# The MLP of a hybrid decoder block: token sums formed from PSUM while the tokens are transposed, three early column pairs, and the down accumulators in the memory of two token sums

## The chip, the core and the metric

The kernel runs on one core of a Trainium2 chip. The metric is device time in microseconds of one execution. The engines are TensorE (PE; its weight loads are shown apart as PEld), VectorE (DVE), ScalarE (ACT), GpSimd (POOL) and SyncE (SP), which only issues DMAs. Each engine works off its own list of instructions in order. A name with a q behind it (ACTq, SPq) in a row is that engine's queue of instructions that are not counted as busy, such as DMA issues.

## The reference

One block over 1024 tokens of width 1024, in float32; the change touches the MLP, and what lies just ahead of it and behind it.

```python
h = x
u = rmsnorm(h, attn_norm_g)
proj = u @ w_in                       # two groups of heads, then a joint projection
...
h = h + mixed @ w_o
v = rmsnorm(h, mlp_norm_g)
hid = square(relu(v @ w_up))          # 1024 -> 4096
h = h + hid @ w_down                  # 4096 -> 1024
out = rmsnorm(h, final_norm_g)
```

## The kernel before

**Precision.** Each float32 operand is split into a rounded high part (an ACT cast, L1079) and the remainder (a subtraction on DVE or POOL, L1080), and a product is the sum of three: high·high, high·low and low·high. The helper `split2` does this pair of operations. Where the source is a 128x512 block the two operations work on 512 columns.

**The MLP in seven products.** The tokens are cut into two halves of 512, the input features into two halves, and w_up into 16 column pairs (NQ); one column pair is two blocks of 128 hidden columns. In place of eight block products a pair takes seven (a Strassen-like scheme in Winograd's form), each of which is one call of `prod`, 12 matmuls of 128x512. The token operands are B11 and B21 (first half of the tokens, lower and upper features), B22 = R22 (second half, upper features) and four sums of token blocks: T1 = R12 − R11, T2 = R22 − T1, T3 = R22 − R12, T4 = R21 − T2. The seven steps of a pair are, by the numbers in the code: 1 and 2 (B11, B21) into one PSUM bank "pa"; 6 (T2) into "pb"; 5 (T1) into "pd"; 7 (T3) into "pc"; 3 (B22) into "pe"; 4 (T4), which goes on top of step 7's bank "pc". Between 7 and 4, DVE has to read "pc" as it stands after step 7 (L1261, written "ho"), so step 4 can't begin before. DVE also forms u from pb and pd. The results go to DRAM (hv_dram, one set for two pairs) and come back for the down projection. The weight combinations S1 to S4 of a pair are formed on DVE (L1204 to L1207) and split by ACT and POOL (`quad_w`).

**The transition from w_o to the MLP.** For each of 8 token tiles t, `wo_ml(t)` finishes the second half of the w_o product (two PSUM tiles "wo_p", read by DVE at L1056) and the norm; `v_tr(t)` transposes the normed tile on PE into two PSUM tiles "vtr" (lower and upper features). For t < 4 these are split into B11 and B21, and a raw copy goes by ACT to a staging tile and to DRAM (r_dram). For t ≥ 4 ACT copies them to R12 and R22. After the last `v_tr`, both r_dram blocks are loaded (L1156, L1157, 1 MB each), and a loop of four column groups of 128 tokens forms the sums (DVE at L1161, L1162, L1164, POOL at L1163) and splits them: per group 5 ACT casts and 5 subtractions of 128x512, three on DVE and two on POOL. To fill PE meanwhile, steps 1 and 2 of the first NPRE = 6 column pairs are taken out of their pairs: `pre_one(q)` is step 1, `pre_two(q)` step 2. Between them ACT has to copy the bank (p1, L1123), since step 2 accumulates on it.

**The start of down.** `down(c)` runs 8 chunks; each has seven products of 4 banks of 6 matmuls ("dn"), and DVE adds every bank to one of four accumulators of 128x2048 in SBUF (L1485), which first have to be loaded with h from DRAM. The accumulators are tiles of a pool that opens when the memory of the token sums and of the hidden tiles is free, so their 16 loads of 256 KB, issued on ACT's queue (L1418), follow the last of these. The work that remains of the last two pairs (`post3`, `post4`, 12 DVE operations) stands ahead of the first accumulation on DVE.

**Order.** PE runs in the order in which the code is written. On the other engines a list scheduler of the framework orders the instructions; a tile that takes the place of another in a pool waits for its last reader.

## Time and profile before

| | |
|---|---|
| time of 3 runs, median | 1229.22 us (1232.68, 1229.09, 1229.22) |
| the profiled execution's own time | 1229.61 us, of which the span of the records is 1227.9 us |
| PE busy | 1156.8 us, 94% of the span, 5424 matmuls |
| DVE, ACT, POOL busy | 946.5, 534.0, 650.3 us |
| mean DMA rate | 146 GB/s |
| mean granted TensorE clock | 0.986 |

The span is the time from the first to the last record of the profiled execution; 1.7 us of its time lie outside. A busy share is a mean over stretches that have different limits: PE is busy 94% of the time on average, and what is left is not spread evenly.

### The profile page before, as it was taken

The page shows a single profiled execution, that of the slowest core. Times are in us where ns is not written, and L with a number is a line of the kernel's source. Part 1 is how long each engine was busy: PE and PEld are TensorE (multiplying, and loading weights), DVE is VectorE, ACT ScalarE, POOL GpSimd, SP SyncE. Part 2 cuts the span into 40 slices and gives each one's busy share as a digit, 9 for nine tenths or more (in the row PEclk, how much of TensorE's full clock was granted, in tenths as well). Part 3 has the DMA queues.
Part 4 walks back from the last instruction along what each step waited for, and adds up shares of the span by engine and source line. Part 5 has one row for each costly group of instructions (what it writes and reads, how often), then busy time and mean ns, then how long its engine had stood idle before and what let it go on. Part 6 is the DMA issues. An engine that isn't in the chain of part 4 may idle for free. (4 is left out here: it accounts for less than half of the span.)

```text
span 1227.9 us, 15872 instructions
## 1 busy us (share of the span) xinstructions
PE 1156.8 (94%) x5424; PEld 942.6 (77%) x5424; DVE 946.5 (77%) x1262; ACT 534.0 (43%) x1080; POOL 650.3 (53%) x539
## 2 busy tenths in 40 slices
PE   9998989888889999999689999999989999999996
PEld 8886876666668888888467788888767888888885
DVE  7686489898987874453979967566498999888995
ACT  6434466676766771245422222322213333333344
POOL 3333454446643452222755655556446966667668
PEclk9999999999999999999989999999999999999998
DMA  6424834342722225475246544443586635454313
GB/s 215 128 63 158 219 82 94 79 99 60 199 80 91 69 83 185 162 248 173 93 139 210 199 148 162 154 155 129 200 299 212 198 123 165 166 171 148 110 52 137
DMA packets 101584, 179.85 MB, mean 146 GB/s; under 512 B 9216, under 2 KB 53760, under 8 KB 100736
## 3 DMA queue, kind: packets, MB, share of 16 engines
q1 hardware_dynamic: 99200, 174.65, 44.5%
q10 hardware_dynamic: 2304, 4.20, 1.0%
q8 instruction: 43, 0.70, 0.2%
q14 instruction: 37, 0.30, 0.1%
HBM read 111.70 MB, written 54.53 MB: 135 GB/s over the span
## 5 line engine op out<-in xcount | busy, mean ns | idle before, releaser
L1481 PE MATMUL dn<-s,s 128*128 128x512 f32 x1344 | 307.3, 391 | 5.0 <-DVE acc L1485 4.3
L1481 PEld LDWEIGHTS dn<-s,s 128*128 128x128 f32 x1344 | 253.2, 189 | 58.9 <-issue 4.7
L1080 POOL TENSOR_TENSOR s<-ar,s 128x1024 fp32r<-128x1024 f32 x56 | 150.3, 2689 | 79.7 <-ACT s L1079 79.7
L1080 POOL TENSOR_TENSOR s<-s,s 128x512 fp32r<-128x512 f32 x84 | 117.0, 1414 | 110.4 <-ACT s L1079 110.4
L1485 DVE TENSOR_TENSOR acc<-acc,dn 128x512 f32<-128x512 f32 x224 | 143.0, 678 | 27.4 <-PE dn L1481 27.4
L1079 ACT CAST s<-wr 128x1024 fp32r<-128x1024 f32 x48 | 50.4, 1051 | 139.0 <-PE dn L1481 97.7
L1086 PE MATMUL pa<-b,s 128*128 128x512 f32 x384 | 93.9, 397 | 7.2 <-ACT p L1123 2.7
L1079 ACT CAST s<-s 128x512 fp32r<-128x512 f32 x84 | 48.3, 620 | 103.1 <-DVE s L1204 58.9
L1086 PEld LDWEIGHTS pa<-b,s 128*128 128x128 f32 x384 | 72.7, 191 | 24.5 <-ACT p L1123 3.1
L488 PE MATMUL mm<-xh,wt 128*128 128x512 f32 x256 | 87.9, 395 | 0.0
L542 POOL TENSOR_TENSOR b<-b,w 128x512 f32<-128x512 f32 (+2 forms) x57 | 58.8, 1032 | 51.4 <-DVE w L536 37.3
L1080 POOL TENSOR_TENSOR s<-wr,s 128x1024 fp32r<-128x1024 f32 x24 | 60.5, 2523 | 28.1 <-ACT s L1079 28.1
L549 PE MATMUL tr<-zid,b 128*128 128x128 f32 x288 | 52.4, 284 | 23.3 <-DVE al L559 13.1
L549 PEld LDWEIGHTS tr<-zid,b 128*128 128x128 f32 x288 | 36.5, 143 | 46.7 <-DVE al L559 23.1
L536 DVE TENSOR_TENSOR_SCAN w<-w,zid 128x129 f32<-128x129 f32 (+1 forms) x64 | 68.5, 1074 | 3.2 <-ACT w L531 2.7
L1079 ACT CAST s<-ar 128x1024 fp32r<-128x1024 f32 x56 | 58.6, 1047 | 25.0 <-DMA acc<-h_dram 16.1
L263 PE MATMUL acc<-wt,xh 128*128 128x448 f32 (+1 forms) x256 | 63.8, 385 | 1.2 <-ACT xh L214 1.2
L1086 PE MATMUL pb<-t,s 128*128 128x512 f32 x192 | 49.9, 408 | 10.4 <-ACT s L1079 9.1
L1080 DVE TENSOR_TENSOR s<-wr,s 128x1024 fp32r<-128x1024 f32 x24 | 53.5, 2230 | 6.9 <-ACT s L1079 6.9
L263 PEld LDWEIGHTS acc<-wt,xh 128*128 128x128 f32 x256 | 49.1, 193 | 8.5 <-ACT xh L214 1.5
L488 PEld LDWEIGHTS mm<-xh,wt 128*128 128x128 f32 x256 | 48.2, 189 | 8.3 <-issue 0.2
L1117 DVE SCALAR_TENSOR_TENSOR ho<-ho 128x512 f32<-128x512 f32 x48 | 52.2, 1088 | 1.4
(330 smaller groups left out, 2672.1 us busy)
## 6 DMA issues: line engine op xcount, KB each, us to landing
ar<-hv_dram SPq DMA_DIRECT2D x56, 512.0 KB, 3.7
s<-in_w_up_dram SPq DMA_DIRECT2D x32, 512.0 KB, 4.7
hv_dram<-s SPq DMA_DIRECT2D x64, 256.0 KB, 2.1
wr<-in_w_down_dram SPq DMA_DIRECT2D x16, 1024.0 KB, 6.3
hv_dram<-ho SPq DMA_DIRECT2D x48, 256.0 KB, 2.1
wr<-in_w_in_dram SPq DMA_DIRECT2D x24, 256.0 KB, 2.9
raw<-in_w_o_dram SPq DMA_DIRECT2D x8, 512.0 KB, 3.5
ht<-h_dram SPq DMA_DIRECT2D x8, 512.0 KB, 4.2
```

The costliest lines, as they stand in the source:

```text
L263: nc.tensor.matmul(accs[t][:, :width], a[:, kk, t * P:(t + 1) * P], wts[kk][:, b, :width], start=(kk == 0 and p == 0), stop=done)
L488: nc.tensor.matmul(ps[:], wt[:, a, k % 4, :], b[:, k, tsl], start=(n == 0), stop=(n == 3 * ND - 1))
L536: nc.vector.tensor_tensor_scan(rv, rv, inject, init, ALU.mult, ALU.add)
L542: eng.tensor_mul(b[:, :n], b[:, :n], w[:, 1:n + 1])
L549: nc.tensor.transpose(tr[:, j * P:(j + 1) * P], sb_a[h, Q, C, j][:, s * P:(s + 1) * P], identf[:])
L1079: nc.scalar.copy(hi, src)
L1080: eng.tensor_sub(lo, src, f(hi))
L1086: nc.tensor.matmul(ps, w[:, a, k, :], bv[:, b, k, :], start=start and n == 0, stop=n == last, skip_group_check=True)
L1117: nc.vector.scalar_tensor_tensor(dst, src, 0.0, src, ALU.max, ALU.mult)
L1481: nc.tensor.matmul(ps[:], av[:, a, u, q * P:(q + 1) * P], bv[i][:, b, u], start=i in (1, 2, 7) and n == 0, stop=n == 5, skip_group_check=True)
L1485: read = nc.vector.tensor_add(dst, dst, ps[:])
```

## The change

Raw blocks stay in SBUF, and the token sums are formed as the tokens are transposed. For t < 4 ACT copies the PSUM tile to L1 or L4 (the raw R11, R21). For t ≥ 4 DVE subtracts straight from PSUM: L1 becomes T1 (L1074), L2 becomes T2 (L1077), L3 becomes T3 (L1078, over an ACT copy of R12 in the same tile); ACT copies R22 to two tiles LB. X = T4 = L4 − L2 is left for later (L1298). The copies to DRAM and back are gone. The sums are then split in five calls of `token_sum`, each of two ACT casts and two DVE subtractions of 128x1024 (10 and 10 in all, none on POOL), and the low parts take the memory of raw blocks that have been read. NPRE is 3 in place of 6. The pools change accordingly: "vtr" has 3 banks in place of 2, "wo_p" 2 in place of 3, the o tiles are 7 in place of 9.

At the start of down, accumulators 11 and 21 take the memory of the high parts of T2 and T1, accumulators 22 and 12 that of their low parts. Their 16 loads are issued on SP as soon as the last products with T2 and T1 are done. `post3` and `post4` of the last two pairs are written after the third product (i = 6) of the first down chunk.

```diff
-    vt_ps = ... name="vt_ps", bufs=2
-    wo_ps = ... name="wo_ps", bufs=3
+    vt_ps = ... name="vt_ps", bufs=3
+    wo_ps = ... name="wo_ps", bufs=2
...
-    R12, R22 = [vraw_pool.tile([P, HD, HT], F32, name=n_) for n_ in ("r12", "r22")]
-    r_dram = [dram.tile([P, HD, HT], F32, name=f"r_dram{n_}") for n_ in range(2)]
+    L1, L3 = [lo_pool.tile([P, HD, HT], F32, name=n_, tag=n_) for n_ in ("l1", "l3")]
+    L2, L4 = [om_pool.tile([P, HD, HT], F32, name=n_, tag=g_) for n_, g_ in (("l2", "om0"), ("l4", "om1"))]
+    LB = [om_pool.tile([P, 2, HT], F32, name="lb0", tag="ssq_m"), lo_pool.tile([P, 2, HT], F32, name="lb1", tag="lb1")]
...
                 split_out(tr[:], bb[:, 0, :, c], bb[:, 1, :, c])
-                stg = vraw_pool.tile([P, HD, P], F32, name="stg", tag="stg", bufs=3)
-                nc.scalar.copy(stg[:], tr[:])
-                nc.sync.dma_start(r_dram[dq][:, :, c], stg[:])
+                nc.scalar.copy((L1, L4)[dq][:, :, c], tr[:])
+            elif dq == 0:
+                nc.vector.tensor_sub(L1[:, :, c], tr[:], L1[:, :, c])
+                nc.scalar.copy(L3[:, :, c], tr[:])
             else:
-                nc.scalar.copy((R12, R22)[dq][:, :, c], tr[:])
+                nc.vector.tensor_sub(L2[:, :, c], tr[:], L1[:, :, c])
+                nc.vector.tensor_sub(L3[:, :, c], tr[:], L3[:, :, c])
+                for g in range(2):
+                    nc.scalar.copy(LB[g][:, :, c], tr[:, 2 * g:2 * g + 2])
...
-    NPRE = 6
+    NPRE = 3
...
     pre_one(0)
+    v_tr(NT - 2)
     pre_one(1)
-    v_tr(NT - 2)
+    v_tr(NT - 1)
     pre_two(0)
+    pre_one(2)
     pre_two(1)
-    pre_w(3)
-    v_tr(NT - 1)
+    pre_two(2)
...
-    nc.sync.dma_start(f(T1[:, 1]), r_dram[0][:])
-    nc.sync.dma_start(f(T4[:, 1]), r_dram[1][:])
-    for j in range(4):
...
+    def token_sum(his, los, raws):
+        for g in range(2):
+            split2(his[g], los[g], raws[g], nc.vector)
+        return lambda b, k: (his, los)[b][k // 2][:, k % 2, :]
...
     weights(0, 3)
+    for g in range(2):
+        nc.vector.tensor_sub(X[:, 2 * g:2 * g + 2], L4[:, 2 * g:2 * g + 2], L2[:, 2 * g:2 * g + 2])
...
+    T2 = token_sum(by_two(H2), by_two(low(om_pool, "om1")), by_two(L2))
+    T1 = token_sum(by_two(H1), by_two(low(om_pool, "om0")), by_two(L1))
+    T3 = token_sum(by_two(H3), by_two(low(lo_pool, "l1")), by_two(L3))
+    B22 = token_sum(by_two(HB), by_two(low(lo_pool, "l3")), [LB[0][:], LB[1][:]])
...
-    quads(last2, (5, 7, 3, 4))
+    quads(last2, (5,))
+    acc = {11: f(v8([P, 4, 512])), 21: f(v8([P, 4, 512]))}
+    for k_, rows, cols in ((11, 0, 0), (21, 4, 0)):
+        for q in range(4):
+            nc.sync.dma_start(acc[k_][:, q], h_dram[q + rows][:, cols:cols + 512])
+    quads(last2, (7, 3, 4))
+    for v, (k_, rows, cols) in enumerate(((22, 4, 512), (12, 0, 512))):
+        acc[k_] = om_pool.tile([P, 4, 512], F32, name=f"acc{k_}", tag=f"om{1 - v}")
+        for q in range(4):
+            nc.sync.dma_start(acc[k_][:, q], h_dram[q + rows][:, cols:cols + 512])
...
-    for q in last2:
-        post3(q)
-        post4(q)
...
-    def load_acc():
...
+            if c == 0 and i == 6:
+                for q in last2:
+                    post3(q)
+                    post4(q)
```

On PE, the end of the w_o product and the start of the MLP stand as follows before the change. A row "vtr" is one `v_tr`, "pa" one product of step 1 (operand b_5719, which is B11) or step 2 (b_5720, B21), "pb" step 6, and s_… the split weights of a pair.

```order
L1068 MATMUL vtr<-zid,junk 128x128 x8
L1086 MATMUL pa<-b_5719,s_6046 128x512 x12
L1086 MATMUL pa<-b_5719,s_6053 128x512 x12
L1068 MATMUL vtr<-zid,junk 128x128 x8
L1086 MATMUL pa<-b_5720,s_6046 128x512 x12
L1086 MATMUL pa<-b_5720,s_6053 128x512 x12
L1068 MATMUL vtr<-zid,junk 128x128 x8
L1086 MATMUL pa<-b_5719,s_6060 128x512 x12
L1086 MATMUL pa<-b_5719,s_6239 128x512 x12
L1086 MATMUL pa<-b_5720,s_6060 128x512 x12
L1086 MATMUL pa<-b_5720,s_6239 128x512 x12
```

The last `v_tr` stands behind four products, and eight follow it before the first product with T2. With the change the same place on PE reads so (b_5723 is B11, b_5724 is B21; v_6291 and low_om_6324 are the high and the low part of T2):

```order
L1068 MATMUL vtr<-zid,junk 128x128 x8
L1093 MATMUL pa<-b_5723,s_5979 128x512 x12
L1068 MATMUL vtr<-zid,junk 128x128 x8
L1093 MATMUL pa<-b_5723,s_6040 128x512 x12
L1068 MATMUL vtr<-zid,junk 128x128 x8
L1093 MATMUL pa<-b_5724,s_5979 128x512 x12
L1093 MATMUL pa<-b_5723,s_6101 128x512 x12
L1093 MATMUL pa<-b_5724,s_6040 128x512 x12
L1093 MATMUL pa<-b_5724,s_6101 128x512 x12
L1093 MATMUL pb<-v_6291,s_6312 128x512
L1093 MATMUL pb<-low_om_6324,s_6312 128x512
```

The last `v_tr` has moved ahead of two of the four products, and four, not eight, stand between it and the first product with T2.

On DVE the work behind the last `v_tr` (its L1077 and L1078 are the two rows ahead of these) is, with the change, two subtractions for X, then the low parts of T2, T1, T3, B22 and T4 one after the other, with the squares (L1139) of the early pairs between:

```order
L1298 TENSOR_TENSOR t4r<-l_5728,l_5727 128x1024 x2
L1139 TENSOR_TENSOR ho<-ho 128x512
L1084 TENSOR_TENSOR low_om_6324<-l_5727,v_6291 128x1024 x2
L1084 TENSOR_TENSOR low_om_6329<-l_5725,v_6292 128x1024 x2
L1139 TENSOR_TENSOR ho<-ho 128x512
L1084 TENSOR_TENSOR low_l_6334<-l_5726,h_6293 128x1024 x2
L1139 TENSOR_TENSOR ho<-ho 128x512
L1084 TENSOR_TENSOR low_l_6339<-lb_5729,hb 128x1024
L1084 TENSOR_TENSOR low_l_6339<-lb_5730,hb 128x1024
L1084 TENSOR_TENSOR low_ssq_m<-t4r,h_6295 128x1024
L1084 TENSOR_TENSOR low_lb_6345<-t4r,h_6296 128x1024
L1246 TENSOR_TENSOR u_6377<-pb,p_6173 128x512
```

What was a loop over column groups, in which all five sums became ready together with the fourth group, is now a list in which they become ready one by one in the order in which PE reads them; the first result of a pair (L1246) stands behind all of it.

At the start of down, DVE's list before the change reads so (s_… <-ho and L1117 are `post3` and `post4`, L1080 a low part of the down weights, L1485 the accumulation):

```order
L1288 TENSOR_TENSOR s_8639<-ho 128x512
L1080 TENSOR_TENSOR s_8626<-t_8608,s_8626 128x1024
L1291 TENSOR_TENSOR s_8641<-s_8637,ho 128x512
L1117 SCALAR_TENSOR_TENSOR ho<-ho 128x512
L1300 TENSOR_TENSOR s_8644<-ho,s_8641 128x512
L1285 TENSOR_TENSOR s_8647<-ho 128x512
L1288 TENSOR_TENSOR s_8649<-ho 128x512
L1291 TENSOR_TENSOR s_8651<-s_8647,ho 128x512
L1485 TENSOR_TENSOR acc_8680<-acc_8680,dn 128x512
L1300 TENSOR_TENSOR s_8654<-ho,s_8651 128x512
L1485 TENSOR_TENSOR acc_8680<-acc_8680,dn 128x512 x7
```

With the change (L1278, L1281, L1284 and L1293 are `post3` and `post4`, v_8478 is accumulator 11, L1481 the accumulation):

```order
L1388 TENSOR_TENSOR wr<-wr 128x2x512
L1278 TENSOR_TENSOR s_8714<-ho 128x512
L1389 TENSOR_TENSOR t_8588<-wr 128x1024
L1391 TENSOR_TENSOR wr<-wr 128x2x512
L1481 TENSOR_TENSOR v_8478<-v_8478,dn 128x512
L1084 TENSOR_TENSOR s_8606<-t_8588,s_8606 128x1024
L1481 TENSOR_TENSOR v_8478<-v_8478,dn 128x512 x5
L1281 TENSOR_TENSOR s_8716<-ho 128x512
L1284 TENSOR_TENSOR s_8718<-s_8714,ho 128x512
L1481 TENSOR_TENSOR v_8478<-v_8478,dn 128x512
L1293 TENSOR_TENSOR s_8721<-ho,s_8718 128x512
```

The first accumulation has moved ahead of `post3` and `post4` but for one operation, and these now lie between accumulations.

## Rows read from the trace of the kernel before

**Rows 1.** The page, busy time and instructions of each engine.

```profile
PE 1156.8 (94%) x5424; PEld 942.6 (77%) x5424; DVE 946.5 (77%) x1262; ACT 534.0 (43%) x1080; POOL 650.3 (53%) x539
```

**Rows 2.** Windows: stretch, length; busy PE, PEld, DVE, ACT, POOL; clock; DMA share, GB/s.

```profile
610.00:615.00 5.00, 0.59 (x3) 0.16 (x1) 3.81 (x8) 2.29 (x6) 1.80 (x1) 0.76 0.25 91
615.00:620.00 5.00, 1.27 (x3) 0.55 (x3) 3.59 (x4) 2.21 (x4) 3.09 (x3) 0.50 0.56 167
```

**Rows 3.** PE timeline of the transition: start, us, what, [idle before, releaser].

```profile
565.84 5.73 PE L1086 MATMUL pa<-b,s 128*128 128x512 f32 x24
...
578.55 11.61 PE L1086 MATMUL pa<-b,s 128*128 128x512 f32 x50
...
607.57 3.02 PE L1086 MATMUL pa<-b,s 128*128 128x512 f32 x12 [2.71 <-ACT p L1123]
618.60 5.27 PE L1086 MATMUL pb<-t,s 128*128 128x512 f32 x12 [8.01 <-ACT s L1079]
623.71 2.96 PE L1086 MATMUL pd<-t,s 128*128 128x512 f32 x12
626.51 2.96 PE L1086 MATMUL pc<-t,s 128*128 128x512 f32 x12
```

**Rows 4.** PE timeline, the two later waits of the up products.

```profile
646.67 3.06 PE L1086 MATMUL pc<-t,a 128*128 128x512 f32 x12 [0.39 <-DVE ho L1261]
...
704.27 3.05 PE L1086 MATMUL pc<-t,a 128*128 128x512 f32 x12 [1.34 <-DVE ho L1261]
```

**Rows 5.** PE timeline, start of down.

```profile
904.41 11.06 PE L1481 MATMUL dn<-s,s 128*128 128x512 f32 x48
919.79 18.43 PE L1481 MATMUL dn<-s,s 128*128 128x512 f32 x73 [4.32 <-DVE acc L1485]
938.94 21.41 PE L1481 MATMUL dn<-s,s 128*128 128x512 f32 x92 [0.72 <-POOL s L1080]
```

**Rows 6.** Window of the steady stretch of down.

```profile
950.00:1190.00 240.00, 240.00 (x1060) 198.82 (x1059) 216.59 (x229) 88.14 (x88) 165.50 (x65) 1.00 0.45 146
```

**Rows 7.** DVE timeline of the transition.

```profile
581.99 2.93 DVE L1161 TENSOR_TENSOR s<-r,t 128x512 f32<-128x512 f32 x2 [2.71 <-DMA t<-r_dram]
...
595.02 6.83 DVE L1080 TENSOR_TENSOR t<-s,t 128x512 fp32r<-128x512 f32 x4
...
605.87 0.68 DVE L1080 TENSOR_TENSOR t<-s,t 128x512 fp32r<-128x512 f32 x1
606.47 0.68 DVE L1164 TENSOR_TENSOR s<-t,s 128x512 f32<-128x512 f32 x1
```

**Rows 8.** POOL timeline of the transition.

```profile
581.36 6.42 POOL L1080 TENSOR_TENSOR b<-r,b 128x512 fp32r<-128x512 f32 x4
```

**Rows 9.** DVE at line L1485: ns min/median/max, first and last start.

```profile
L1485 DVE TENSOR_TENSOR acc<-acc,dn x224: 672/675/689, 919.0 to 1219.6; 128x512 f32<-128x512 f32 x112
```

**Rows 10.** DVE timeline, operations of 128x1024, and the start of down.

```profile
892.58 3.43 DVE L1080 TENSOR_TENSOR s<-wr,s 128x1024 fp32r<-128x1024 f32 x1
...
908.09 1.22 DVE L1375 TENSOR_TENSOR wr<-wr 128x1024 f32<-128x1024 f32 x1
909.22 0.68 DVE L1288 TENSOR_TENSOR s<-ho 128x512 f32<-128x512 f32 x1
...
918.97 0.68 DVE L1485 TENSOR_TENSOR acc<-acc,dn 128x512 f32<-128x512 f32 x1
```

**Rows 11.** ACT timeline, start of down.

```profile
910.51 16.72 ACTq L1418 DMA_DIRECT2D acc<-h_dram  x9
927.27 1.05 ACT L1079 CAST s<-ar 128x1024 fp32r<-128x1024 f32 x1 [16.05 <-DMA acc<-h_dram]
```

**Rows 12.** The accumulators' loads at L1418, from issue to landing.

```profile
DMA to landing us min/median/max: 3.0/5.3/7.2
```

**Rows 13.** PE and DVE timelines, one half of a w_o token tile.

```profile
549.35 1.56 PE L967 MATMUL wo_p<-s,oml 128*128 128x512 f32 x6
...
550.67 0.74 DVE L1056 SCALAR_TENSOR_TENSOR ht<-wo_p,rs_mla,ht 128x512 f32<-128x512 f32 x1
```

More of the change, by code (lines that the diff above doesn't have):

```diff
@@ L796, in tile_hymba_block @@
     om_pool = om_stack.enter_context(tc.tile_pool(name="om_pool", bufs=1, reuse_waits="tile"))
-    o_mla = om_pool.tile([P, MH, T], F32, name="o_mla")
-    ssq_m = om_pool.tile([P, T], F32, name="ssq_m")
+    o_mla = [om_pool.tile([P, 2, T], F32, name=f"o_mla{e}", tag=f"om{e}") for e in range(2)]
+    ssq_m = om_pool.tile([P, T], F32, name="ssq_m", tag="ssq_m")
     rs_sb = om_pool.tile([P, NT], F32, name="rs_sb")
@@ L1028, in o_tile @@
     def o_tile(nm):
-        return o_pool.tile([P, 512], F32, name=nm, tag="o", bufs=9)
+        return o_pool.tile([P, 512], F32, name=nm, tag="o", bufs=7)
+    lo_pool = ctx.enter_context(tc.tile_pool(name="lo_pool", bufs=1, side="right", reuse_waits="tile"))
     va_stack = ExitStack()
@@ L1080, in split2, with whole @@
         eng.tensor_sub(lo, src, f(hi))
+    def whole(t):
+        return lambda b, k: t[:, b, k, :]
     def prod(ps, w, bv, start, stop):
@@ L1085, in prod @@
             for a, b in ((0, 0), (0, 1), (1, 0)):
-                nc.tensor.matmul(ps, w[:, a, k, :], bv[:, b, k, :], start=start and n == 0, stop=n == last,
+                nc.tensor.matmul(ps, w[:, a, k, :], bv(b, k), start=start and n == 0, stop=n == last,
                                  skip_group_check=True)
@@ L1092, in col_block @@
         return w_up[:, c0:c0 + P].rearrange("(k p) f -> p k f", p=P)
-    NPRE = 6
+    NPRE = 3
+    V11, V21 = whole(B11), whole(B21)
     x_of, p1_of = {}, {}
@@ L1127, in pre_two @@
         p1, ps = p1_of[q]
-        prod(ps[:], x_of[q][:, 1], B21, False, True)
+        prod(ps[:], x_of[q][:, 1], V21, False, True)
         hid = o_tile("ho")
@@ L1137, in tile_hymba_block @@
             v_tr(t - 2)
-        if t == NT - 3:
-            for q in range(3):
-                pre_w(q)
+        if t >= NT - 4 and t < NT - 1:
+            pre_w(t - NT + 4)
     pre_one(0)
+    v_tr(NT - 2)
     pre_one(1)
-    v_tr(NT - 2)
+    v_tr(NT - 1)
     pre_two(0)
+    pre_one(2)
     pre_two(1)
-    pre_w(3)
-    v_tr(NT - 1)
+    pre_two(2)
     wo_stack.close()
-    om_stack.close()
-    v8_stack.close()
-    rope_stack.close()
+    for s_ in (rope_stack, v8_stack, om_stack):
+        ctx.enter_context(s_)
     bcd_ps = mlp_psum.enter_context(tc.tile_pool(name="bcd_ps", bufs=5, space=PSUM, reuse_waits="tile"))
@@ L1303, in tile_hymba_block, with low @@
     weights(0, 3)
+    for g in range(2):
+        nc.vector.tensor_sub(X[:, 2 * g:2 * g + 2], L4[:, 2 * g:2 * g + 2], L2[:, 2 * g:2 * g + 2])
+    def low(pool, tag, shape=(P, HD, HT)):
+        return pool.tile(list(shape), F32R, name="low_" + tag, tag=tag)
+    T2 = token_sum(by_two(H2), by_two(low(om_pool, "om1")), by_two(L2))
+    T1 = token_sum(by_two(H1), by_two(low(om_pool, "om0")), by_two(L1))
+    T3 = token_sum(by_two(H3), by_two(low(lo_pool, "l1")), by_two(L3))
+    B22 = token_sum(by_two(HB), by_two(low(lo_pool, "l3")), [LB[0][:], LB[1][:]])
+    T4 = token_sum([H4[0][:], H4[1][:]], [low(om_pool, "ssq_m", (P, 2, HT))[:], low(lo_pool, "lb1", (P, 2, HT))[:]], by_two(X))
+    tmp_stack.close()
+    o2_stack = ExitStack()
+    o2_pool = o2_stack.enter_context(tc.tile_pool(name="o2_pool", bufs=1, reuse_waits="tile"))
     flush()
@@ L1494, in down @@
                         finish(q, read, square(q, 1, dst))
-    for c in range(NCH):
+            if c == 0 and i == 6:
+                for q in last2:
+                    post3(q)
+                    post4(q)
+        if c == 0:
+            flush()
+    down(0)
+    o2_stack.close()
+    vb_stack.close()
+    dn_pool = ctx.enter_context(tc.tile_pool(name="dn_pool", bufs=1, reuse_waits="tile"))
+    fin_pool = ctx.enter_context(tc.tile_pool(name="fin_pool", bufs=1, reuse_waits="tile"))
+    gfb = rope_pool.tile([P, D], F32, name="gfb", tag="ssq_s")
+    ys = [fin_pool.tile([P, D], F32, name=f"y{n_}") for n_ in range(4)]
+    fss = [fin_pool.tile([P, 4], F32, name=f"fss{n_}") for n_ in range(NT)]
+    sqj = fin_pool.tile([P, 512], F32, name="sqj")
+    for c in range(1, NCH):
         down(c)
```

68 lines of the change are left out of this document (17 added, 51 removed).

## The prediction

> **What bounds the kernel now.** The page comes first: PE is busy for 1156.8 of 1227.9 us [rows 1]. In such a kernel an edit on another engine pays only where PE stands still, so the next view is PE's own timeline around the two places that the change touches.
>
> The transition from w_o to the MLP: PE does four products in line (565.84 and after), the last tokens are transposed by 578.55, and from there to 623.71 it does nine products [rows 3]. A product in line takes 626.51 − 623.71 = 2.80 us [rows 3], so nine are 25.2 of these 45.16 us: **20.0 us are lost**. The row at 618.60 shows the largest piece, 8.01 us of waiting for an ACT cast, and 5.27 us for 12 matmuls; the windows say why that is more than 2.80: the clock granted between 615 and 620 is 0.50, that is 1.2 instead of 2.4 GHz, behind a window in which PE was busy for 0.59 of 5 us and DVE for 3.81 [rows 2]. What PE waits for are the token sums and the weights behind them on the same engines. DVE's operations show why they are late: it stands still 2.71 us for the reload from r_dram, and while POOL works beside it a 128x512 subtraction takes 6.83 / 4 = 1.71 us, against 0.68 when it is alone (and 0.60 from start to start) [rows 7]; POOL's own take 1.6 [rows 8]. Two later waits of up products, 0.39 and 1.34 us [rows 4], come from the same backlog on DVE: 1.7 more.
>
> The start of down: 48 + 73 matmuls fill 904.41 to 938.94 [rows 5]. In the steady stretch 1060 take 240 us, 0.2264 each [rows 6], so 121 would take 27.4 of these 34.5: **7.1 us lost**. PE waits for the first accumulation, which DVE starts at 918.97 [rows 10], 14 us after the first bank was begun; ACT's queue is busy with issuing accumulator loads for 16.72 us, and its next cast waits 16.05 for one of them [rows 11]. Each lands 5.3 us after its issue [rows 12]; what is late is the issue, since the memory is free only behind the last hidden work.
>
> So 20.0 + 1.7 + 7.1 = 28.8 us can be had, no more, as far as these two places go.
>
> **The transition, part by part.** Moved on PE: pairs 3 to 5 do steps 1 and 2 in their pairs again; the number of products stays. Between 565.84 and 578.55 lie four products and two v_tr [rows 3]; 12.7 less 4 × 2.8 leaves 0.75 for each v_tr. With one product ahead of v_tr(6) and one between the two, v_tr(7) ends at 565.84 + 2 × 2.8 + 2 × 0.75 = about 573.0 instead of 578.55. Four products follow, to 584.2, and then PE wants T2, and T1, T3, B22, T4 each 2.8 us later: the last at 595.4.
>
> Removed: 8 stores, 2 loads of 1 MB, DVE's wait of 2.71, and the POOL share of the sums. The sums T1, T2, T3 come out of DVE's reads of PSUM: three 128x512 subtractions for each t ≥ 4 in place of ACT copies. Their nearest row is L1485, a subtraction's twin with one operand in PSUM: 224 of them between 672 and 689 ns, with POOL at work during most [rows 9, 6]. I take 0.60 from start to start; the upper bound is 1.7 each, if reading PSUM did not help.
>
> DVE's list from the end of v_tr(6), about 569.6, on: 7 of these subtractions, 4 weight combinations of pair 0, 3 squares: 14 × 0.60 = 8.4. Two for X and ten low parts of 128x1024 at 909.22 − 908.09 = 1.13 [rows 10]: 13.6. The end is at 591.6 if nothing disturbs it. POOL has only five splits of 128x512 in this time (pair 0's weights), and each can cost DVE 1.71 − 0.68 = 1.0 us at most: I take 4, the range is 0 to 5. So T4's low part is ready at about 595.6, and PE wants it at 595.4: the list just keeps ahead of PE, since the sums come in the order of their use. T2's low part has 11 short operations, two for X, a square and itself ahead, 12 × 0.60 + 4 × 1.13 = 11.7, so it is there at 581.3 for 584.2.
>
> ACT has ten casts of 128x1024 at 1.05 [rows 11], 10.5 us, where there were 20 of half the size; it isn't the bound. But step 2 of pair 2 waits for the copy p1, which stands behind the first casts in ACT's list; the same kind of wait cost 2.71 at 607.57 [rows 3]. I take 1.6 (0 to 3).
>
> What is late next is the bank pc. Step 4 of pair 0 may start only when DVE has read pc (L1254). That stands behind all low parts and four more operations: 595.6 + 5 × 0.6 = 598.6, against 595.4 + 1.6 on PE: 1.6, and with the clock after a pause 2.5 (1.5 to 5). The next pairs inherit some of it: 1 (0 to 2), as before [rows 4]. Residue 1.6 + 2.5 + 1 = 5.1. **Gain 20.0 + 1.7 − 5.1 = 16.6.**
>
> Costed at nothing: "wo_p" with two banks. A bank is needed again two halves later. A half is 12 matmuls, 2.8 us of PE, and DVE's read at 550.67 is that of the half before, which ended at 549.35: 1.3 behind, done 2.1 behind [rows 13]. With two banks it may be done 2.8 behind, or 3.6 where a v_tr lies between. If the three subtractions (1.8 us) always stood ahead of this read, PE would wait 2.1 + 1.8 − 3.6 = 0.3 in each of four tiles; I leave 1 us of it to the range. Fewer o tiles: no row shows a wait for one; their readers stand soon behind their writers.
>
> **The start of down, part by part.** Sixteen loads move from ACT's queue to SP's, free to go when T2 and T1 have been read for the last time, which is six products (steps 7, 3, 4 of two pairs), 16.8 us, ahead of down's first matmul. With 5.3 us from issue to landing [rows 12] accumulators 11 and 21, the first eight, are there when DVE wants to add the first bank; 22 and 12 are wanted only from the fourth product on. On SP nothing stands behind them but the `ar` loads of later products and the stores of `post3` and `post4`. `post3` and `post4` lie between accumulations: at most 11 operations of 0.6 are 6.6 us of DVE, which has 7 products of 5.4 us (24 matmuls × 0.2264) with four accumulations of 0.60 each, that is 3 us free per product. So the 4.32 goes, and the rest mostly: residue 1 (0 to 2.5), since the splits of the first products (POOL, the 0.72 at 938.94) stay as they are [rows 5]. **Gain 6.1.**
>
> **Sum.** 16.6 + 6.1 = 22.7. The profiled execution took 1229.6, so 1206.9; that execution lies 0.4 above the median of 1229.2, so I say **1206.5**. With the bounds of the residues (from 1.5 to 13.5 us in all, the 1 for POOL's fifth split and for wo_p among the latter) the forecast's own range is 1202 to 1214.
>
> **Rivals.**
>
> *DVE crawls (chance 0.12).* If DVE falls to 1.7 us for 128x512 beside POOL for the whole list, not for five operations, then T4 comes late. POOL has also pair 1's splits; nine POOL operations at 1.2 each are 10.8 more, most of it seen by PE: 1217. For it: all of DVE's new work behind the transposes has both inputs in SBUF, like the 1.71 us rows and the 3.43 us of a 128x1024 one at 892.58 [rows 7, 10]. Against it: pair 1's ACT casts stand behind the casts of the sums, so POOL has nothing to do for most of the list. The Trainium skill (SBUF — State Buffer, section "SBUF: two separate sides") says that a DVE operation with two SBUF inputs and a GpSimd operation that reads SBUF take a shared port in turn, each for a whole instruction. The trace agrees: 0.68 alone, 1.71 beside POOL, and 0.67 to 0.69 with a PSUM operand. By that rule the transposes' subtractions can't suffer, and only the twelve long operations can, by up to one POOL operation each.
>
> *The start of down stays (0.08).* If the loads come late behind SP's other work, or a DVE list in which `post3` is slowed (0.68 is not the only price there), PE waits for the accumulators as before: of the 6.1 nothing is left, 1212.5.
>
> *Opposite sign: two wo_p banks (0.03).* If DVE's reads in the last token tiles are later than the 2.8 to 3.6 us that two banks allow, PE waits in each half. With 16 halves it needs 22.7 / 16 = 1.4 us of waiting in each to eat the gain, that is a lag of about 4.6 us on average; the row shows 2.1, and only four tiles get more work. Beyond that the kernel is slower, 1232 or more.
>
> *The change doesn't do what it says (0.03).* If the list scheduler's order on DVE made the sums as late as before, the time would stay at 1229. The order shows them in the sequence of use, so I give it little.
>
> **How the numbers follow.** Forecast 0.74, the rivals 0.12, 0.08, 0.03, 0.03. The range has to leave out at most 2 in 10: from 1200.5 (1229.2 less all of the 28.8) to 1215, which takes in the forecast, the down rival and part of the crawl. Faster by over 0.3% (3.7 us, about what a measurement of this kernel can tell from no change): 0.94; within 0.3%: 0.03; slower: 0.03.
>
> **What would show it.** In the profile of the changed kernel: DVE's operations at L1074, L1077 and L1078 at 0.68 whatever POOL does; the low parts (L1084, 128x1024) at 1.2 with few at 2 or more; the first product with T2 right behind the four, about 18 us after v_tr(6) begins; at most three waits of 1 to 3 us from there to the second pair; clock 1.00 in all windows of that stretch; the first accumulation 2 to 4 us behind the first matmul of down, and no ACT wait for accumulators. Wrong I would be if the low parts take 2 us and more, if PE waits for wo_p, or if the time between the two places, all of which I take as unchanged, moves.

## The result, and the profile after

The changed kernel takes **1210.94 us** (median of 4 runs, 1209.87 to 1214.13) against 1229.89 us (4 runs of before, 1229.09 to 1232.68); the ratio is 0.9854 with a 95% interval of 0.9839 to 0.9869. That is 19 us less, clear of the 0.3% that can be told here. The forecast was 1206.5 with a range of 1200.5 to 1215: the sign and the range held, the point was 4.4 us too low. The profiled execution took 1209.87 us with a span of 1207.7.

The first part of the page, busy time by engine; it answers to [rows 1]:

```profile
PE 1150.3 (95%) x5424; PEld 941.1 (78%) x5424; DVE 923.2 (76%) x1259; ACT 531.8 (44%) x1074; POOL 633.2 (52%) x530
```

PE is busy 6.5 us less with the same 5424 matmuls, a first sign that more than waits has changed.

PE's timeline of the transition; it answers to [rows 3] and [rows 4]:

```profile
564.65 3.01 PE L1093 MATMUL pa<-b,s 128*128 128x512 f32 x12
...
571.92 11.18 PE L1093 MATMUL pa<-b,s 128*128 128x512 f32 x48
582.93 0.39 PE L1093 MATMUL pb<-v,s 128*128 128x512 f32 x1
...
593.89 0.40 PE L1093 MATMUL pe<-hb,s 128*128 128x512 f32 x1
597.96 0.76 PE L1093 MATMUL pc<-h,a 128*128 128x512 f32 x1 [3.67 <-DVE ho L1254]
...
613.98 0.50 PE L1093 MATMUL pc<-h,a 128*128 128x512 f32 x1 [0.46 <-DVE ho L1254]
...
630.12 0.50 PE L1093 MATMUL pc<-h,a 128*128 128x512 f32 x1 [2.00 <-DVE ho L1254]
...
632.99 2.92 PE L1093 MATMUL pa<-b,s 128*128 128x512 f32 x12
```

The reader is to see that the four early products run on without a gap into T2's (582.93), that the wait of 8.01 us is gone, and that what is left stands ahead of step 4 of pairs 0, 1 and 2, each time for the same DVE line, the read of bank pc. From 582.93 to 632.99 PE does 15 products, 42.0 us at 2.80, in 50.06: 8.1 us lost, where before 20.0 + 1.7 were.

Windows of 5 us of the same stretch (columns as in [rows 2]):

```profile
575.00:580.00 5.00, 5.00 (x24) 4.11 (x22) 5.00 (x5) 5.00 (x10) 5.00 (x3) 1.00 0.01 3
...
590.00:595.00 5.00, 4.29 (x18) 2.93 (x16) 5.00 (x6) 0.00 (x0) 0.00 (x0) 1.00 0.34 105
595.00:600.00 5.00, 2.04 (x5) 1.68 (x6) 5.00 (x8) 1.70 (x3) 1.98 (x2) 0.78 0.80 254
600.00:605.00 5.00, 5.00 (x21) 4.04 (x20) 4.93 (x5) 1.30 (x3) 5.00 (x4) 0.88 0.30 112
```

DVE, the third of the busy times, has next to no idle time; between 590 and 595 it is the only engine beside PE that works. Behind PE's pause the granted clock is 0.78 and 0.88, means over a part of each window at the lower level (1.2 GHz) and the rest at the upper one (2.4 GHz); PE had stood still for 3.67 us before.

DVE's timeline there; it answers to [rows 7]:

```profile
574.61 0.68 DVE L1077 TENSOR_TENSOR l<-vtr,l 128x512 f32<-128x512 f32 x1
575.21 0.68 DVE L1078 TENSOR_TENSOR l<-vtr,l 128x512 f32<-128x512 f32 x1
575.81 3.45 DVE L1298 TENSOR_TENSOR t4r<-l,l 128x1024 f32<-128x1024 f32 x2
579.18 1.78 DVE L1139 TENSOR_TENSOR ho<-ho 128x512 f32<-128x512 f32 x1
580.89 4.81 DVE L1084 TENSOR_TENSOR low_om<-l,v 128x1024 fp32r<-128x1024 f32 x4
...
593.60 1.22 DVE L1084 TENSOR_TENSOR low_lb<-t4r,h 128x1024 fp32r<-128x1024 f32 x1
...
597.13 0.68 DVE L1254 TENSOR_TENSOR ho<-pc,u 128x512 f32<-128x512 f32 x1
```

The subtractions from PSUM take 0.68, the low parts 1.2 each, and in this list only X and two squares (1.78 in place of 0.68) are slowed. The last low part ends at 594.8; L1254 comes behind it and four more operations, as forecast.

The start of down, PE and then DVE; it answers to [rows 5] and [rows 10]:

```profile
886.83 22.19 PE L1477 MATMUL dn<-s,s 128*128 128x512 f32 x97
911.98 48.20 PE L1477 MATMUL dn<-s,s 128*128 128x512 f32 x204 [2.96 <-DVE s L1084]
```

```profile
892.18 0.68 DVE L1481 TENSOR_TENSOR v<-v,dn 128x512 f32<-128x512 f32 x1
...
896.90 2.27 DVE L1281 TENSOR_TENSOR s<-ho 128x512 f32<-128x512 f32 x1
899.10 2.89 DVE L1284 TENSOR_TENSOR s<-s,ho 128x512 f32<-128x512 f32 x1
901.91 0.68 DVE L1481 TENSOR_TENSOR v<-v,dn 128x512 f32<-128x512 f32 x1
902.51 2.28 DVE L1293 TENSOR_TENSOR s<-ho,s 128x512 f32<-128x512 f32 x1
...
910.71 1.21 DVE L1084 TENSOR_TENSOR s<-wr,s 128x1024 fp32r<-128x1024 f32 x1
```

The first accumulation starts 5.4 us behind the first down matmul, not 14. But a new wait stands behind 97 matmuls: the low part of the fifth product's weights (910.71) is late, because three operations of `post3` and `post4` ahead of it take 2.3 to 2.9 us each.

**The account.** PE's own records split the span into four: up to the first up product, from there to the first down matmul, from there to the last down matmul's start, and the rest.

| | before | after | difference |
|---|---|---|---|
| up to the first up product | 565.8 | 564.7 | −1.2 |
| up products | 338.6 | 322.2 | −16.4 |
| down matmuls | 311.9 | 309.4 | −2.5 |
| behind them | 11.6 | 11.5 | −0.1 |

In the twelve experiments' profiles the first up product starts between 562.7 and 566.9 us, so the first row is no gain of the change. The second row is firm: where nothing in the up products was edited (runs 1, 7 and 10 below) the stretch is 322.1 to 322.2 again. The third is less so: with the changed kernel's start of down it is 308.8 to 310.5 in seven executions, and before the change it is 311.9 here, 311.8 and 310.3 in runs 8 and 4, which leave down as it was.

No run puts back the trip through DRAM alone or the loop over column groups alone. That DVE's wait for the reload [rows 7] is a part of what was lost is read from the trace of before, not shown by an experiment.

### The profile page after: what moved, and what is told of

Same layout as the page of the kernel before. It is cut to its first block, busy times and chain, and to the rows that moved or that the text cites. A ratio compares the mean times of both kernels' runs of the same rounds, so it can differ in the third digit from the quotient of the medians.

```text
span 1207.7 us, 15834 instructions
## 1 busy us (share of the span) xinstructions
PE 1150.3 (95%) x5424; PEld 941.1 (78%) x5424; DVE 923.2 (76%) x1259; ACT 531.8 (44%) x1074; POOL 633.2 (52%) x530
## 5 line engine op out<-in xcount | busy, mean ns | idle before, releaser
L1084 POOL TENSOR_TENSOR s<-s,s 128x512 fp32r<-128x512 f32 x90 | 130.0, 1468 | 122.2 <-ACT s L1083 122.2
L1083 ACT CAST s<-s 128x512 fp32r<-128x512 f32 x90 | 51.8, 619 | 100.0 <-DVE s L1197 62.7
L1481 DVE TENSOR_TENSOR v<-v,dn 128x512 f32<-128x512 f32 x128 | 80.9, 676 | 3.4 <-PE dn L1477 3.4
L1481 DVE TENSOR_TENSOR acc<-acc,dn 128x512 f32<-128x512 f32 x96 | 63.7, 681 | 24.5 <-PE dn L1477 24.5
L1197 DVE TENSOR_TENSOR s<-s 128x512 f32<-128x512 f32 x16 | 11.1, 691 | 60.3 <-POOL a L1084 60.3
```

The lines of the kernel that those rows point to most:

```text
L1083: nc.scalar.copy(hi, src)
L1084: eng.tensor_sub(lo, src, f(hi))
L1197: nc.vector.tensor_add(r22, r21, r22)
L1481: read = nc.vector.tensor_add(dst, dst, ps[:])
```

## The experiments

The first three undo a part of the change or move work to another engine, and the rest try reasons; **u** and **d** are the up and down rows of that table, each from one execution. The kernel before, measured again beside runs 1 to 4, 5 to 8 and 9 to 12, has medians of 1230.36, 1230.31 and 1229.07 us against 1229.89 above, so times of different groups compare to about 1 us.

**1. `post3` and `post4` ahead of down again.**

```diff
+    for q in last2:
+        post3(q)
+        post4(q)
+    flush()
     mlp_psum.close()
...
-            if c == 0 and i == 6:
-                for q in last2:
-                    post3(q)
-                    post4(q)
-        if c == 0:
-            flush()
```

> Of the changed kernel one thing is undone: the twelve operations of post3 and post4 stand ahead of down again; the early accumulator loads stay. Theory A (DVE's list bounds the start of down, whatever the loads do): the first accumulations come 8 to 10 us later, PE stands still about 4 us behind its first 48 down matmuls as it did before the change, the wait of 3.35 us behind 96 matmuls goes; from the first to the last down matmul 311 to 312 us instead of 309.4, the time 1212 to 1214. Rival (the late loads alone were the trouble): the down stretch stays at 309.4 or falls, the time stays at 1210 to 1211.

Measured: 1214.32 us (1207.96 to 1216.65, the widest spread of all runs), u 322.1, d 312.8. PE's timeline:

```profile
887.53 11.08 PE L1481 MATMUL dn<-s,s 128*128 128x512 f32 x48
905.07 25.25 PE L1481 MATMUL dn<-s,s 128*128 128x512 f32 x103 [6.46 <-DVE v L1485]
```

The wait behind the first 48 matmuls is back, 6.46 us and so longer than expected. The times overlap with those of the changed kernel and don't show the loss by themselves; d does. With early loads alone the start of down is no better than before the change (d 311.9); theory A stands, the order on DVE decides.

**2. The transposes late again.**

```diff
     pre_one(0)
-    v_tr(NT - 2)
     pre_one(1)
-    v_tr(NT - 1)
+    v_tr(NT - 2)
     pre_two(0)
-    pre_one(2)
     pre_two(1)
+    v_tr(NT - 1)
+    pre_one(2)
     pre_two(2)
```

> Of the changed kernel only PE's order is undone: the last two transposes stand behind two and four of the early products, as before the change; what is computed where stays. Theory (DVE's list behind the last transpose sets when pair 0 can go on): that list starts 5.6 us later for its long operations, its end moves by 3 to 5 us, and so does the wait ahead of step 4 of pair 0 (3.67 us now): the time 1214 to 1216. Rival (the list has slack, the place of the transposes doesn't matter): the wait stays below 4.5 us, the time within 1 us of 1210.9.

Measured: 1210.69 us (1210.24 to 1211.31), u 323.0, d 308.8. **The theory fell** on the time. Two lines of PE's and two of DVE's timeline:

```profile
583.66 3.04 PE L1093 MATMUL pa<-b,s 128*128 128x512 f32 x12 [1.70 <-ACT p L1131]
...
600.87 0.47 PE L1093 MATMUL pc<-h,a 128*128 128x512 f32 x1 [2.66 <-DVE ho L1254]
```

```profile
587.16 0.68 DVE L1198 TENSOR_TENSOR s<-s 128x512 f32<-128x512 f32 x1
...
597.51 1.21 DVE L1084 TENSOR_TENSOR low_lb<-t4r,h 128x1024 fp32r<-128x1024 f32 x1
```

The list of low parts does end late (598.7, not 594.8; PE itself is 0.5 later in this run). But four operations which in the changed kernel stand behind the list (three weight combinations of pair 1, L1197 to L1199, and L1246) are now done within it, and POOL's splits of pair 0 were over when X came, so that it takes 2.34 in place of 3.45. PE in turn reached step 4 later, since it had waited 0.86 and 1.70 us for the copies p1: its waits from the first up product to the third pair's step 4 add up to 6.3 us, against 6.1 in the changed kernel. The rival's signs came. My reading is that what counts is not when the list of sums ends but the sum of DVE's work up to the third pair.

**3. Four of the ten low parts on POOL.**

```diff
...
-    T3 = token_sum(by_two(H3), by_two(low(lo_pool, "l1")), by_two(L3))
-    B22 = token_sum(by_two(HB), by_two(low(lo_pool, "l3")), [LB[0][:], LB[1][:]])
+    T3 = token_sum(by_two(H3), by_two(low(lo_pool, "l1")), by_two(L3), nc.gpsimd)
+    B22 = token_sum(by_two(HB), by_two(low(lo_pool, "l3")), [LB[0][:], LB[1][:]], nc.gpsimd)
```

> Of the changed kernel the four low parts of T3 and B22 (128x1024 each) go to POOL, which stands idle in that stretch; six stay on DVE. Theory (DVE and POOL take turns on operands that all lie in SBUF): DVE's remaining long operations grow from 1.2 us to 2.4 and more while POOL works, little or nothing is gained; the time 1210 to 1214. Rival (two engines share the work): DVE's list ends 4.5 us earlier, the wait of 3.67 us ahead of step 4 of pair 0 goes; the time 1206 to 1207.

Measured: 1215.63 us (1212.46 to 1217.14), u 328.4, 6.2 us more. DVE's, POOL's and PE's timeline:

```profile
595.82 3.38 DVE L1084 TENSOR_TENSOR low_ssq_m<-t4r,h 128x1024 fp32r<-128x1024 f32 x1 [4.71 <-POOL low_l L1084]
```

```profile
587.81 5.53 POOL L1084 TENSOR_TENSOR low_l<-l,h 128x1024 fp32r<-128x1024 f32 x2 [5.42 <-ACT ho L1138]
593.42 4.70 POOL L1084 TENSOR_TENSOR low_l<-lb,hb 128x1024 fp32r<-128x1024 f32 x2
```

```profile
606.97 0.77 PE L1093 MATMUL pc<-h,a 128*128 128x512 f32 x1 [7.37 <-DVE ho L1254]
```

POOL takes 2.77 for what DVE does in 1.2, DVE's own part beside it takes 3.38, and step 4 waits 7.37. Split in this way, the work takes longer: 4.7 us by the medians. But the run does not show that taking turns is the whole reason. Ahead of its next long operation DVE stands idle for 4.71 us, because that operation (low_ssq_m) takes the memory of a raw block that POOL is still reading, until the first of the two at 593.42 is done. So a part of the loss is a chain through memory, and a split of the work without that chain is untested.

**4. The kernel before, with its token-sum tiles moved by 128 bytes.** T1's and T2's products take 2.72 us after the change, T3's and B22's 2.79 to 2.80. One with T2 runs from 635.75 to the next product's start:

```profile
635.75 0.39 PE L1093 MATMUL pb<-v,s 128*128 128x512 f32 x1
...
638.47 2.88 PE L1093 MATMUL pa<-b,s 128*128 128x512 f32 x12
```

The compiler's addresses show one difference: all operands of products at 2.72 start 224 bytes behind a multiple of 256, T1 and T2 after the change among them; the token sums of before start at 96, and after the change the high parts of T3 and B22 at 32.

```diff
+    vb_pool.tile([P, 32], F32, name="shift")
     T2, T1, T3, B22, T4 = [vb_pool.tile([P, 2, HD, HT], F32R, name=n_) ...
```

> The kernel before the change with one edit: an unused strip of 128 bytes per partition ahead of the five token-sum tiles, so that their rows start 128 bytes later. Theory (where in 256 bytes the moving operand starts decides between 0.2267 and 0.233 us for one 128x512 matmul, since T1 and T2 gained that much in the changed kernel when their start moved from 96 to 224 bytes behind a multiple of 256): all 80 products with a token sum fall from 2.80 to 2.72 us, the time of before falls by 5 to 6.5 us, to 1223.5 to 1225. Rival (T1 and T2 gained by another thing, such as high and low part in tiles of their own): products stay at 2.80 us, the time within 1.5 us of 1229.9.

Measured: 1225.51 us (1225.38 to 1227.16) against 1230.36, ratio 0.9966 (0.9953 to 0.9979). PE's timeline, and that of run 8 (below, 160 bytes) at the same place of the program:

```profile
749.43 2.88 PE L1086 MATMUL pb<-t,s 128*128 128x512 f32 x12
752.15 2.88 PE L1086 MATMUL pa<-b,s 128*128 128x512 f32 x12
```

```profile
745.52 2.97 PE L1086 MATMUL pb<-t,s 128*128 128x512 f32 x12
748.32 2.92 PE L1086 MATMUL pa<-b,s 128*128 128x512 f32 x12
```

From start to start 2.72 against 2.80: an unused strip of 128 bytes makes every such product 0.08 us shorter. The time fell by 4.9, a little less than the 5 to 6.5 expected, but the profile doesn't let all of it be put down to the products. They save 6.2 us (80 at 0.08), yet u is 336.3 and only 2.3 shorter than before: the waits ahead of step 4 at 646 and 704 are 0.6 and 0.7 us longer, and more matmuls run at the lower clock, as behind the second of these waits, where the granted clock from 705 to 710 is 0.66 and was 1.00. Another 1.7 us of this execution lie in d (310.3), which the strip was not meant to touch.

**5. Four early pairs.**

```diff
-    NPRE = 3
+    NPRE = 4
...
     pre_two(1)
+    pre_one(3)
     pre_two(2)
+    pre_two(3)
```

> Of the changed kernel NPRE becomes 4: one more pair's steps 1 and 2 (two products, 5.6 us of PE) stand ahead of the first product with T2. The runs before put down what is left of the transition's loss (8.1 us of PE standing still or slowed ahead of step 4 of pairs 0 to 2) to DVE, which has no idle from 575 to 620. Theory (a backlog of DVE work): PE's extra products give DVE 5.6 us for one more square, the waits ahead of step 4 shrink to 2 to 4 us in all; the time 1205 to 1208. Rival (the splits of one more pair's weights and its p1 copy cost as much, or the waits follow other things): the time within 1.5 us of 1210.9 or above.

Measured: 1206.68 us (1204.92 to 1209.82), u 318.7, 3.5 less; d 310.5. PE's timeline:

```profile
604.66 0.47 PE L1093 MATMUL pc<-h,a 128*128 128x512 f32 x1 [1.52 <-DVE ho L1256]
...
648.22 0.50 PE L1093 MATMUL pc<-h,a 128*128 128x512 f32 x1 [1.80 <-DVE ho L1256]
```

The backlog theory holds: two more products for PE, one more square for DVE, and the waits shrink to 4.3 us (these two and one of 1.0 for a copy p1) from 6.1. The slowed matmuls behind the first wait, 1.5 us, are gone too. Three early pairs are one too few for the time.

**6. The changed kernel with T3's and B22's high parts moved by 192 bytes.**

```diff
+    vb_pool.tile([P, 48], F32, name="shift")
     H3, HB = [vb_pool.tile([P, HD, HT], F32R, name=n_) for n_ in ("h3", "hb")]
```

> Of the changed kernel only the place of the high parts of T3, B22 and of half of T4 is moved, by an unused strip of 192 bytes, so that they start 224 bytes behind a multiple of 256 as T1, T2, B11 and B21 do; the first half of T4's high part stays at 96. Theory (start of the moving operand): products of steps 7 and 3 fall from 2.79 to 2.72 us, step 4 by about half of that; 16 pairs make 2 to 3 us, the time 1208 to 1209.5. Rival (what T1 and T2 gained came with the memory they lie in): steps 7 and 3 stay at 2.79 us.

Measured: 1210.31 us (1208.15 to 1211.14), u 320.8, 1.4 less. Steps 7 and 3 fall to 2.72 us, as said; the time can't be told from that of the changed kernel, so only the mechanism is shown by this run, not a gain.

**7. `post3` and `post4` spread.**

```diff
-            if c == 0 and i == 6:
-                for q in last2:
-                    post3(q)
-                    post4(q)
+            if c == 0 and i in (6, 7, 5, 4):
+                (post3 if i in (6, 5) else post4)(last2[i in (5, 4)])
```

> Of the changed kernel the operations of post3 and post4 are spread: a third or so behind each of the third to sixth products of the first down chunk instead of all behind the third. Theory (the wait of 3.35 us at the fifth down product is DVE's list: three of these operations take 2.3 to 2.9 us each beside POOL and stand ahead of the low part that the fifth product wants): the wait falls below 1.5 us, the down stretch from 309.4 to 306.5 to 308; the time 1208.5 to 1210. Rival (DVE is short by the same sum wherever they stand): the wait moves to a later product, the stretch stays within 0.7 us.

Measured: **1218.73 us** (1216.78 to 1222.19), d 316.6, a miss of both theories. The wait of 2.96 us ahead of the fifth product goes, and the sixth waits 0.99 for another engine, but behind 168 matmuls there is a new one:

```profile
932.45 0.80 PE L1477 MATMUL dn<-s,s 128*128 128x512 f32 x1 [6.35 <-ACT s L1083]
```

```profile
931.36 1.04 ACT L1083 CAST s<-wr 128x1024 fp32r<-128x1024 f32 x1 [16.34 <-DMA wr<-in_w_down_dram]
```

The second chunk's weights come late, because SP issues their load late, at 920.27 against 911.67 in the changed kernel:

```profile
920.27 1.41 SPq L1345 DMA_DIRECT2D wr<-in_w_down_dram  x3
```

The last operation of `post4` ends 4.8 us later than there (915.6 against 910.8), and the load stands behind its store on SP. For the rest SP waits for POOL, the longest time (4.7 us) for an `ar` load ahead of it in its list. How much of the 8.6 us is memory that comes free late, and how much is SP's order, the trace doesn't separate.

**8. The kernel before, moved by 160 bytes** (the diff of 4 with 40 in place of 32), one run.

> The kernel before the change with a strip of 160 bytes in place of 128, so that the token-sum tiles start at a multiple of 256 bytes. If only the start 224 bytes behind such a multiple is quick (all other operands lie there), products stay at 2.79 to 2.80 us; if what counts is that the operand starts in the last or first part of such a block, they take 2.72.

Products stay at 2.80 (rows above); the up stretch is 338.9 and no shorter than before. A start at a multiple of 256 is slow too. The one time, 1226.69 us, is still 3.6 below the median of before in its group (1230.31): its first up product starts 3.1 us earlier, at 562.7. So a difference of 3 to 4 us in a single run says nothing about the products.

**9. Sums from SBUF copies, not from PSUM.**

```diff
-                nc.vector.tensor_sub(L1[:, :, c], tr[:], L1[:, :, c])
                 nc.scalar.copy(L3[:, :, c], tr[:])
+                nc.vector.tensor_sub(L1[:, :, c], L3[:, :, c], L1[:, :, c])
...
+                    nc.vector.tensor_sub(L2[:, k_, c], LB[g][:, :, c], L1[:, k_, c])
+                    nc.vector.tensor_sub(L3[:, k_, c], LB[g][:, :, c], L3[:, k_, c])
```

> Of the changed kernel one thing is undone: the token sums of the last four token tiles are formed from the raw copies that ACT has put into SBUF (the same tiles as before, T2 and T3 in halves of 128x256), not from PSUM. Theory (reading PSUM keeps these subtractions at 0.68 us while POOL splits weights, and DVE's list is a backlog that PE sees): some of them take 1.2 to 1.8 us and wait for the ACT copies, the list ends 2 to 4 us later, the time 1212.5 to 1215. Rival (their source doesn't matter, since DVE had slack before the last transpose): within 1 us of 1210.9.

Measured: 1214.8 us (1214.21 to 1215.92), u 329.0, 6.9 more. DVE's and PE's timeline:

```profile
576.21 1.51 DVE L1081 TENSOR_TENSOR l<-lb,l 128x256 f32<-128x256 f32 x1
...
580.51 0.41 DVE L1082 TENSOR_TENSOR l<-lb,l 128x256 f32<-128x256 f32 x1
```

```profile
582.20 4.49 PE L1095 MATMUL pa<-b,s 128*128 128x512 f32 x12 [2.39 <-ACT p L1133]
...
600.98 0.77 PE L1095 MATMUL pc<-h,a 128*128 128x512 f32 x1 [3.07 <-DVE ho L1256]
```

Half a block takes 1.51 us beside POOL and 0.41 without, a whole one from PSUM 0.68 at the same place. ACT's casts then wait for the sums, the early products wait 2.39 us for the copy p1 behind these casts, and a product after that wait takes 4.49 us in place of 2.9. Forming the sums from PSUM is worth some 4 us of the time; in that stand the source, the wait for ACT's copies that it saves, and whole blocks in place of halves, which this run does not separate.

**10. The accumulators' loads late, on ACT's queue.**

```diff
-            nc.sync.dma_start(acc[k_][:, q], h_dram[q + rows][:, cols:cols + 512])
...
+                    with tc.issue_after(st[NQ - 1]["end"].ins):
+                        nc.scalar.dma_start(acc[k_][:, q], h_dram[q + rows][:, cols:cols + 512])
```

> Of the changed kernel only the accumulators' 16 loads are undone: they are issued on ACT's queue behind the last up product, into the same memory; post3 and post4 stay behind the third down product. Theory (both parts are needed: early loads, and accumulations ahead of post3 and post4): the first accumulation waits for a load, ACT's casts wait behind the issues, PE stands still 4 to 8 us in the first five products; the down stretch 313 to 317 us instead of 309.4, the time 1214 to 1218. Rival (only the order of post3 and post4 counts): the stretch stays below 310.5.

Measured: 1213.97 us (1212.37 to 1214.9), d 311.9. Half right. The accumulators were there in time, the scheduler having put the issues further up in ACT's list: the first is at 865.93, where the changed kernel has 864.82. So the loads were not late after all, and the run tests the queue alone. PE waits 1.20 and 4.07 us, not for the accumulators but for DVE, whose work is late because ACT's casts stand behind the issues, as ACT's timeline shows:

```profile
865.93 0.34 ACTq L1451 DMA_DIRECT2D acc<-h_dram  x1
...
876.84 1.05 ACT L1083 CAST s<-ar 128x1024 fp32r<-128x1024 f32 x1 [13.31 <-DMA v<-h_dram]
```

So two things are needed, the order of `post3` and `post4` and a queue without casts: without either of them d is 312 to 313, with both 308.8 to 310.5. What the early hour of the loads is worth by itself no run shows.

**11. Runs 5 and 6 together**, with both diffs.

> The changed kernel with four early pairs and with the strip of 192 bytes ahead of the high parts of T3 and B22. If the two gains add (4.3 us and 0.6 to 2 us): 1204 to 1206. If what the quicker products save is waited for ahead of step 4 instead: 1206 to 1207.

1206.43 us (1205.72 to 1207.47), u 318.5: the gains do not add, the up stretch is that of run 5 (318.7). The products are quicker, as in run 6. The waits ahead of step 4 are only 0.4 us longer than in run 5; most of the saving goes to matmuls at the lower clock behind two waits (granted clock 0.73 from 645 to 650 and 0.77 from 860 to 865, where run 5 has 1.00 in both). So the time is as the second of the two expectations has it, and the way only in small part.

**12. Run 11, and the fourth product's hidden operand cast ahead of the third's weights.**

```diff
-    for i in DORD[:4]:
-        pre_ab[i] = split_a(ar0[i])
...
+    for i in DORD[:2]:
+        pre_ab[i] = (split_a(ar0[i]), prep0(i))
+    av_ = {i: split_a(ar0[i]) for i in DORD[2:4]}
+    for i in DORD[2:4]:
+        with tc.issue_after(st[NQ - 1]["end"].ins):
+            pre_ab[i] = (av_[i], prep0(i))
```

> As the run before, and at the start of down ACT casts the fourth product's hidden operand ahead of the third product's weights, so that POOL splits it while DVE is still at weights and not beside post3. Theory (POOL's splits make three operations of post3 and post4 take 2.3 to 2.9 us, and this makes the fifth product late): the wait of 3.3 us ahead of the fifth down product falls by 1 to 2.5 us, the time by as much against the run before, to 1202 to 1205. Rival (those operations meet another split of POOL just the same): within 0.7 us of the run before.

1205.55 us (1205.47 to 1207.03), d 307.6 against 308.9 in run 11. PE's and DVE's timeline:

```profile
907.60 5.73 PE L1479 MATMUL dn<-s,s 128*128 128x512 f32 x24 [1.19 <-DVE s L1084]
```

```profile
894.29 2.27 DVE L1284 TENSOR_TENSOR s<-ho 128x512 f32<-128x512 f32 x1
896.49 0.68 DVE L1287 TENSOR_TENSOR s<-s,ho 128x512 f32<-128x512 f32 x1
```

One of the three slow operations is quick now, in a moment when POOL stands idle (896.0 to 897.5); the other two still take 2.27 and 2.72 beside it. The wait is 1.19 in place of 2.48 in run 11. The stretch gains 1.3 us; between the medians lies 0.9, too little to tell. It is the quickest kernel of the study: ratio to before 0.9816 (0.9794 to 0.9837), some 5 us below the changed kernel.

## Why the prediction was right, and where its sizes were off

**What bounded the kernel.** Right: PE stood still at the two places named, and the gain came from there. The up products took 16.4 us less, the down matmuls 2.5.

**The transition, 16.6 forecast.** By the same account it is 21.7 − 8.1 = 13.6. The order of events came as worked out: early products in line up to 582.93 (584.2 less the 1.2 by which this run was ahead), T4's low part ready at 594.8 (595.6 less 1.2 is 594.4), PSUM reads at 0.68. The residue was 8.1 and not 5.1. The wait for p1 (1.6) did not come, but nothing was won by that: PE was so much earlier at step 4 of pair 0 and waited there instead. That wait was sized at 2.5 and is 3.67 and another 1.5 of slowed matmuls: from 597.96 to 602.30 twelve of them take 4.34 us, not 2.80, in windows whose granted clock is 0.78 and 0.88. And the 1 us for "the next pairs" (0 to 2) is 0.46 + 2.00. The step that was too small here is "the next pairs inherit some of it": it took the list of sums as the thing that PE waits for. The runs bear out that it is DVE's work in sum until about 622, where DVE has its first idle time: moving the transposes changes nothing (run 2), slower sums cost 4 us (run 9), and two more products of PE's give 4 us back (run 5). Run 3, with four low parts on POOL, fits too, but mixes in a wait for memory.

**The start of down, 6.1 forecast.** 2.5 came. The 4.32 for the first accumulation went, as said; the step that failed is that `post3` and `post4` lie between accumulations at 0.6 each. Three of them take 2.3 to 2.9 while POOL, from 893.3 to 904.2, splits the first products' operands without a pause, and the fifth product waits 2.96; seven slow matmuls behind it (granted clock 0.68 from 910 to 915) take 1.6 more. The residue was stated as 1 (0 to 2.5). The trace of before had 2.89 for the same operation, and the prediction priced it by the row of 0.68 [rows 10]:

```profile
910.96 2.89 DVE L1291 TENSOR_TENSOR s<-s,ho 128x512 f32<-128x512 f32 x1
```

That part of the rival on the start of down came true. Runs 1 and 10 show that the order and the queue are both needed; run 12 shows one of the operations at 0.68 where POOL is idle.

**Not foreseen.** T2's and T1's products are 0.07 us shorter by where their operands start: 32 products, 2.2 us, of which 1.8 lie behind 632.99. It was taken for granted that a product is 2.80 us wherever its operands lie; those with B11 and B21 take 2.72 in the trace of before already. With this the up stretch closes. From one matmul's start to the next, steps of more than 0.27 us, waits and slowed matmuls, hold 25.8 us above 0.2266 each before and 11.7 after, 14.1 less; the rest of the stretch is 2.3 shorter. 14.1 + 2.3 is the 16.4.

**The total.** The two sizes were 3.0 and 3.6 us too large. That the point is off by only 4.4 owes some 2 us to the shorter products, and that is luck.

**The signs.** The subtractions from PSUM at 0.68, the low parts at 1.2 and no wait of ACT's for accumulators came. The clock of 1.00 throughout did not, nor did "at most three waits of 1 to 3 us" (3.67, 0.46, 2.00) and a first accumulation 2 to 4 us behind the first matmul (5.4). The first product with T2 comes 15.4 us behind the start of v_tr(6), at 567.50; the 18 in the prediction does not follow from its own times, which give 584.2 − 568.6 = 15.6. And one sign of being wrong came: the time between the two places moved, by the 1.8 us.

**Two banks for "wo_p".** Right: no row of the trace after has PE waiting for L1056.

**The rivals.** That DVE crawls for its whole list did not come: the low parts take 1.2. That single operations would if POOL had work then is shown by two in run 3, 3.38 and 2.29. The prediction held that only the twelve long operations could suffer; the squares, which read SBUF alone, did too. What the Trainium skill says of the shared port (SBUF — State Buffer, section "SBUF: two separate sides"), that a DVE operation with two SBUF inputs and a GpSimd operation that reads SBUF block each other for a whole instruction, agrees with runs 3 and 9: 3.38 us in place of 1.2, and 1.51 in place of 0.41, beside POOL, and 0.68 with a PSUM operand in the changed kernel.

## What to carry to other kernels

When a stall ends, ask which engine has no idle time left around it, and count that engine's work in sum until it has caught up. In run 2 an edit that only changed the order of this work moved the wait and not the time; in run 1 the order cost time, because it put work ahead of what PE wanted sooner, and in run 7, because it made a load late. Give an operation that reads only SBUF the price it has beside POOL if POOL has anything to do at that moment, and form what can be formed while the operand is still in PSUM. A DMA issue that may have to wait for memory doesn't belong on a queue with casts that others wait for, and run 7 suggests that work which a load waits for, by memory or by a queue, should not be put off.
